# The gates of the first 128 tokens: one-hot products on TensorE, or indexed DMAs into a table in HBM

## The chip, the cores and the metric

The kernel runs on one core of one Trainium2 chip. The metric is the device time of one execution in microseconds (us), the median of several runs. TensorE (PE) multiplies matrices, VectorE (DVE) and ScalarE (ACT) work elementwise, GpSimd (POOL) and SyncE (SP) issue DMAs here. A profile row marked PEld is a weight load of TensorE.

## The reference, cut to what matters

A network of a hybrid mixer, an expert layer and two further layers on 256 tokens of width 1024, all in float32. The change is inside the expert layer: 8 heads each choose 16 of 128 x 128 experts for a token, and an expert is one row of `expert_u` and one of `expert_v`.

```python
v_half, i_half = lax.top_k(s, PEER_TOPK)
cand = (v_half[:, :, 0, :, None] + v_half[:, :, 1, None, :]).reshape(T, PEER_HEADS, PEER_TOPK * PEER_TOPK)
best, pos = lax.top_k(cand, PEER_TOPK)
i1 = jnp.take_along_axis(i_half[:, :, 0], pos // PEER_TOPK, axis=-1)
i2 = jnp.take_along_axis(i_half[:, :, 1], pos % PEER_TOPK, axis=-1)
experts = (i1 * PEER_KEYS + i2).reshape(T, PEER_HEADS * PEER_TOPK)
gates = jax.nn.softmax(best, axis=-1).reshape(T, PEER_HEADS * PEER_TOPK).astype(n.dtype)
...
u = expert_u[eb].astype(xb.dtype)
act = jax.nn.gelu(jnp.einsum('td,tkd->tk', xb, u), approximate=False) * gb
return jnp.einsum('tk,tkd->td', act, expert_v[eb].astype(xb.dtype))
```

## The kernel before, in words

All weights stream through the core once, as 523 chunks of 128 x 1024 floats (512 KB). SP issues each load into one of four buffers `raw`. ScalarE rounds it to `wh` and VectorE subtracts, `wl = raw - wh` (`pump_split`, L348); `wh` and `wl` have three buffers each, and the subtraction of a chunk is called its split below. A product is made of three: `wh` with the high part of the activations, `wh` with the low part, `wl` with the high part (`mm_a`, L424). So a chunk in the first expert stage is 24 matmuls of 256 columns, and the next load can be issued when the chunk four before it has been split.

The expert layer does not gather rows. Its **first stage** multiplies all tokens with all of `expert_u`: 128 chunks, one for each first index j, give 128 rows of activations `Hact` (tiles `hactA`, `hactB`), each 128 second indices by 256 tokens. Its **second stage** multiplies `Hact` with all of `expert_v`, again 128 chunks. What makes the result sparse is a gate for each expert and token, zero almost everywhere, by which gelu(`Hact`) is multiplied between the stages.

The gates come from work beside the stream. `topk1` (L1031) ranks the scores of a block of 128 tokens, `topk2` (L1040) ranks the sums, makes the gates `gt` and the two indices `isel`, and three TensorE transposes bring them to `idxT`. `g_side` (L1105) then takes four tokens at a time: ScalarE makes a one-hot tile `oA` of the first index, VectorE one of the second times the gate (`oB`), one float32 product for each token sums the 128 chosen experts into a gate table in PSUM (tile `sm`), and the table goes to `Hact`: where the row of activations is there already, VectorE multiplies it in, and where not, ScalarE copies the gates there, and `u_post` (L1200) multiplies gelu by them later.

`peer_side` (L1157) sets the order: `topk1(0)` and `topk2(0)` of tokens 0 to 127 first, then `g_side(0)` in turn with the ranking of tokens 128 to 255, then `g_side(1)`. Each part yields a cost, and each chunk of the stream grants it a rate, so these numbers pace the work:

```python
yield from paced(topk1(0), 1.3)
yield from paced(topk2(0), 1.3)
...
yield from paced(alternate(g_side(0), second()), 1.4)
yield from paced(g_side(1), 1.6)
```

The layer that records the program then orders each engine's instructions; every engine, and SP's queue, works through its own list in that order. `w_split` (L1231) splits two rows of `Hact` for the second stage.

Of the kernel before, what the change touches and what calls it, by code (L numbers as in the profile page):

```python
# [32 lines left out]
T0 = 16          # column of the first x token in the transposed activations (16 meta tokens precede)  # L33

# packed constants (from shapes alone)
# [3 lines left out]
def _consts():  # L39
# [11 lines left out]
    put("iota", np.broadcast_to(i[None, :], (128, 128)))  # L51
    first = off
# [19 lines left out]
# packed per-partition vectors  # L72
# [10 lines left out]
# the order of the mixer's products: gates (Z), steps (d), the groups of the scan, short convolution (S)  # L83
# [3 lines left out]
def half_order(nq):  # L87
    """The chunks (column half, place among the nq) of an output product before its last three: of a short
    one the second half starts early, as its last rows come late."""
    if nq == 4:  # L90
        return [(0, 0), (0, 1), (1, 0), (0, 2), (0, 3)]
    return [(0, i) for i in range(nq)] + [(1, i) for i in range(nq - 3)]


def layout(inp):
    """Lays the inputs out for the kernel: permutations, copies and concatenations only."""
    g = {k: np.asarray(v) for k, v in inp.items()}

    def A(w, c0):
        # 128 columns from c0, stationary: [128 d, kt, 128]  # L100
        w = w[:, c0:c0 + 128]
        return w.reshape(-1, 128, 128).transpose(1, 0, 2).reshape(128, -1)

    def Bc(w, c0, q):
        # rows of k-tiles 2q, 2q+1, 512 columns from c0
        return w[q * 256:(q + 1) * 256, c0:c0 + 512].reshape(2, 128, 512).transpose(1, 0, 2).reshape(128, 1024)
# [97 lines left out]
def build(tc, a, out):  # L204
    nc = tc.nc
    top = ExitStack()
    with top:
# [5 lines left out]
        # one area for the buffers of all phases, cut by hand (in KiB per partition); row j of the  # L213
        # expert activations lies at j KiB
# [10 lines left out]
        def place(off, shape, dtype, name):  # L225
            """A tile at byte off of the area; it takes over from what lies there."""
# [10 lines left out]
        class Pool:  # L237
            """Cuts [lo, hi) KiB of the area; a name's tiles rotate over its bufs slots."""
# [55 lines left out]
        # ------------------------------------------------------------ first loads  # L294
# [34 lines left out]
        # ------------------------------------------------------------ the weight stream  # L329
# [47 lines left out]
        # ------------------------------------------------------------ work beside the stream  # L377
# [14 lines left out]
        def add_side(gen, rate=1.0):  # L392
            """A generator of work beside the stream: it yields what its last part costs (1 if nothing),
            and gets rate per chunk."""
# [28 lines left out]
        # ------------------------------------------------------------ products with streamed weights  # L423
# [8 lines left out]
        def wa(o, rh, rl, c0, n):  # L432
            """One stationary chunk: o[128 columns, n tokens]."""
# [10 lines left out]
        def wb(outs, xh, xl, k0, c0, first, last):  # L444
            """One moving chunk of two k-tiles: outs[t][128 tokens, 512 columns]."""
# [5 lines left out]
        # ------------------------------------------------------------ norms between the phases  # L451
        def rstd_of(ssq, n, width, np_=128, eps=EPS):
            """1/sqrt(ssq/width + eps) for [128, n] sums."""
# [4 lines left out]
            # h = -v/2; a first guess of v^-1/2 from the bits of v/2, then Newton's iteration to  # L458
            # float32's accuracy
# [18 lines left out]
        def tr_half(z, n, h, l, c0, np_=128):  # L478
            """z[tokens, 512] transposed into k-tiles 4n .. 4n+3 of the two parts."""
# [15 lines left out]
        def start_next(h, l, c0, nh, between):  # L495
            """The first nh chunks of the next phase, the first four k-tiles first."""
# [11 lines left out]
        def scale_of(s2, r):  # L508
            """r[128, 2] = rstd of the sums of the two blocks; returns r by columns on all partitions."""
# [11 lines left out]
        def out_phase(pool, xh, xl, c0, ks, res, sets, nh, rs=None):  # L521
            """res += x^T W (times rs by token) by column halves. The result times the gains of sets is
            transposed into their parts as it comes, and the next phase starts on the first of them; the
            scale of the norm is left to its readers. Returns the first products and the sums of squares."""
# [95 lines left out]
        # ============================================================ hybrid mixer  # L620
# [30 lines left out]
        # the first three chunks of z, one block of tokens after the other  # L651
# [31 lines left out]
        def dt_side(dtr):  # L683
# [17 lines left out]
            # log1p(e) = 2 atanh(z), z = e / (2 + e) in (0, 1/3]  # L701
# [29 lines left out]

        def ssd_group(g):
# [5 lines left out]
            # s0  # L738
# [10 lines left out]
            # s1  # L749
# [22 lines left out]
            # s2  # L772
# [16 lines left out]
            # s3  # L789
# [4 lines left out]
            # s4  # L794
# [6 lines left out]
            # s5  # L801
# [6 lines left out]
            # s6  # L808
# [16 lines left out]
            # s7  # L825
# [4 lines left out]
            # s7, s8  # L830
# [7 lines left out]
            # gate, norm within the group  # L838
# [75 lines left out]
        def sc_chunks(i):  # L914
            # the convolution reaches two tokens back
# [24 lines left out]

        z_chunk()
# [25 lines left out]
        # ============================================================ PEER  # L967
# [6 lines left out]
        def Hact(j0, j1, t0, t1):  # L974
            """Rows j0 .. j1 of the expert activations for tokens t0 .. t1, in pieces: rows and tokens
            from the start of the range, and the piece."""
# [19 lines left out]
        idxT = tp.tile([128, 3, 256], F, name="idxT")  # L996
        ust = {"J": 0, "T": 0, "sc": set(), "topk": -1}
# [42 lines left out]
        def topk2(tb):  # L1040
# [5 lines left out]
            # of the sums of two falling lists only those of ranks r, s with (r + 1)(s + 1) <= 16 can be  # L1046
# [644 lines left out]
```

## Time and profile before

| | us |
|---|---|
| median of three runs (lowest, highest) | 1706.02 (1705.64, 1706.15) |
| span of the profiled execution | 1704.0 |
| first expert stage, about | 281 to 707 |
| block 0's products (tokens 0 to 127) | within 364 to 584 |
| second expert stage, about | 707 to 1107 |

The span runs from the first to the last instruction of the profiled execution; the runs' times hold some 2 us around it. An engine's list is worked through in order, so a row with idle time before it names what the engine waited for. A product of four tokens' one-hot tiles shows as eight records, two for each.

### The profile page before, as it was taken

What the parts mean: (1) busy time and instruction counts of PE and PEld (TensorE: products, weight loads), DVE (VectorE), ACT (ScalarE), POOL (GpSimd) and SP (SyncE); (2) the same over time, 40 slices, a digit from 0 to 9 for tenths busy, and PEclk for the clock granted to TensorE, in tenths of its full rate; (3) what the DMA queues carried; (4) which work ended last, traced back from release to release, by engine and by line L of the source; (5) the groups of instructions that cost most, each with busy time, mean ns of one, the idle gap of its engine ahead of it and who ended that gap; (6) DMA issues with size and microseconds to landing.
All of it is one profiled execution on the core that took longest, in us unless ns stands there. A gap on an engine that the chain in (4) does not pass through costs nothing. (4 is left out here: it accounts for less than half of the span.)

```text
span 1704.0 us, 29681 instructions
## 1 busy us (share of the span) xinstructions
PE 1683.1 (99%) x11373; PEld 1529.4 (90%) x11373; DVE 1271.0 (75%) x2529; ACT 1018.4 (60%) x1784; POOL 0.2 (0%) x4
## 2 busy tenths in 40 slices
PE   8999999999999999999999999999999999999998
PEld 6999889999999999988888888898899988799986
DVE  6789778989985699855555565887787757777754
ACT  6877456568885698644444555733555545665543
POOL 0000000000000000000000000000000000000000
PEclk9999999999999999999999999999999999999999
DMA  6444465554446544455555585533465655256553
GB/s 210 142 132 128 156 214 171 167 180 137 137 154 185 169 149 143 155 185 186 187 192 188 189 311 187 171 123 118 139 191 186 187 176 169 76 171 187 184 183 117
DMA packets 80959, 286.82 MB, mean 168 GB/s; under 512 B 9121, under 2 KB 11681, under 8 KB 80562
## 3 DMA queue, kind: packets, MB, share of 16 engines
q1 hardware_dynamic: 80818, 284.94, 52.8%
q8 instruction: 89, 1.46, 0.3%
q14 instruction: 52, 0.43, 0.1%
HBM read 282.80 MB, written 2.10 MB: 167 GB/s over the span
## 5 line engine op out<-in xcount | busy, mean ns | idle before, releaser
L271 DVE TENSOR_TENSOR wl<-raw,wh 128x1024 fp32r<-128x1024 f32 x523 | 638.7, 1222 | 295.8 <-ACT wh L283 293.4
L283 ACT ACTIVATE wh<-raw 128x1024 fp32r<-128x1024 f32 x523 | 551.7, 1057 | 425.9 <-PE acc L265 404.1
L265 PE MATMUL acc<-xTh,wh 128*128 128x256 f32 (+2 forms) x2184 | 543.9, 287 | 0.2 <-ACT xTh L283 0.2
L265 PE MATMUL acc<-xTl,wh 128*128 128x256 f32 (+2 forms) x2184 | 534.3, 282 | 1.0 <-DVE xTl L271 1.0
L265 PEld LDWEIGHTS acc<-xTl,wh 128*128 128x128 f32 x2184 | 412.5, 189 | 2.5 <-DVE xTl L271 1.2
L265 PEld LDWEIGHTS acc<-xTh,wh 128*128 128x128 f32 x2184 | 411.7, 189 | 3.2 <-issue 1.7
L265 PE MATMUL acc<-xTh,wl 128*128 128x256 f32 (+2 forms) x2184 | 306.8, 281 | 0.0
L265 PEld LDWEIGHTS acc<-xTh,wl 128*128 128x128 f32 x2184 | 279.8, 188 | 0.3 <-issue 0.3
L265 PE MATMUL acc<-wh,wth 128*128 128x512 f32 x512 | 201.8, 394 | 0.0
L265 PE MATMUL acc<-wl,wth 128*128 128x512 f32 x512 | 201.7, 394 | 0.0
L265 PE MATMUL acc<-wh,wtl 128*128 128x512 f32 x512 | 161.7, 394 | 0.0
L265 PEld LDWEIGHTS acc<-wh,wth 128*128 128x128 f32 x512 | 95.7, 187 | 23.9 <-issue 0.3
L265 PEld LDWEIGHTS acc<-wh,wtl 128*128 128x128 f32 x512 | 95.7, 187 | 23.6
L265 PEld LDWEIGHTS acc<-wl,wth 128*128 128x128 f32 x512 | 95.8, 187 | 23.6
L283 ACT ACTIVATE oA<-cst,idxT 128x128 f32<-128x128 f32 x256 | 83.9, 393 | 3.6 <-DVE idxT L1102 2.8
L277 DVE TENSOR_SCALAR oB<-cst,idxT 128x128 f32<-128x128 f32 x256 | 71.5, 341 | 1.1 <-PE sm L265 1.0
L265 PE MATMUL sm<-oB,oA 128*128 128x128 f32 x512 | 68.2, 276 | 4.1 <-DVE sw L1026 2.0
L265 PE MATMUL acc<-wl,fh 128*128 128x512 f32 x176 | 69.4, 394 | 0.0
L265 PE MATMUL acc<-wh,fh 128*128 128x512 f32 x176 | 69.4, 394 | 0.0
L265 PE MATMUL acc<-wh,fl 128*128 128x512 f32 x176 | 69.4, 394 | 0.0
L265 PEld LDWEIGHTS sm<-oB,oA 128*128 128x128 f32 x512 | 62.4, 191 | 5.7 <-ACT hactB L283 5.3
L283 ACT ACTIVATE wth<-hactA 128x512 fp32r<-128x512 f32 x48 | 30.3, 632 | 60.7 <-PE acc L265 58.4
(318 smaller groups left out, 2084.7 us busy)
## 6 DMA issues: line engine op xcount, KB each, us to landing
raw<-in_u SPq DMA_DIRECT2D x128, 512.0 KB, 3.6
raw<-in_v SPq DMA_DIRECT2D x128, 512.0 KB, 3.5
raw<-in_up SPq DMA_DIRECT2D x88, 512.0 KB, 3.6
raw<-in_w_in SPq DMA_DIRECT2D x45, 512.0 KB, 3.6
raw<-in_dn SPq DMA_DIRECT2D x44, 512.0 KB, 3.6
raw<-in_hg_in SPq DMA_DIRECT2D x32, 512.0 KB, 3.6
raw<-in_w_out SPq DMA_DIRECT2D x16, 512.0 KB, 3.6
raw<-in_w_q SPq DMA_DIRECT2D x16, 512.0 KB, 3.8
```

Source lines behind the costliest of these rows:

```text
L265: PE.matmul(o, l, r, start=start, stop=stop_)
L271: V.tensor_tensor(out=o, in0=x, in1=y, op=op)
L277: V.tensor_scalar(o, x, s1, s2, op0=op0, op1=op1)
L283: S.activation(o, i, f, **kw)
```

## The change

Tokens 128 to 255 keep their one-hot products. For tokens 0 to 127 `topk2` computes the place of each gate in a table `gtab` of 128 tokens x 128 x 128 floats in HBM (8 MB), from a new constant column `row`, the token's number. `scatter` issues 128 indexed DMAs on POOL, each of which adds one gate for each token (128 rows of 4 bytes) at its place. The 16 DMAs of a head go to different places; those of a later head may meet the same ones, so a head waits for the head before it. The table is written with zeros during the mixer, in 16 writes of 512 KB on SP (`zero_side`). `u_post` now writes gelu of tokens 0 to 127 straight to `Hact`. `g_load` reads the gates of two rows of `Hact` back (128 x 256 floats, two buffers `gts`), and `w_split` multiplies them in. The ranking of tokens 128 to 255 no longer alternates with products, and the rates change. Comments are left out too.

```diff
+        gtab = dram.tile([128 * 128 * 128, 1], F, name="gtab")
+        gtv = gtab.rearrange("(a c) o -> a (c o)", a=128)
+        zero = m2.tile([128, 256], F, name="zero", bufs=1)
+        V.memset(zero, 0.0)
+        def zero_side():
+            for i in range(16):
+                yield
+                SP.dma_start(gtv[:, i * 1024:(i + 1) * 1024].rearrange("a (k c) -> a k c", k=4),
+                             zero[:, None, :].to_broadcast([128, 4, 256]))
...
+        add_side(zero_side(), 0.5)
...
-        ust = {"J": 0, "T": 0, "sc": set(), "topk": -1}
+        gplace = tp.tile([128, 128], I32, name="gplace")
+        gval = tp.tile([128, 8, 16], F, name="gval")
+        ust = {"J": 0, "T": 128, "sc": set(), "topk": -1}
...
-            gt = tp.tile([128, 8, 16], F, name="gt")
+            gt = gval if tb == 0 else tp.tile([128, 8, 16], F, name="gt")
...
+            if tb == 0:
+                pl = ihf.rearrange("p (s h) r -> p s (h r)", s=2)[:, 0]
+                flat = lambda t: t.rearrange("p h r -> p (h r)")
+                ts(pl, flat(isel[:, 0]), -16384.0, C("row"), OP.mult, OP.add)
+                stt(gplace, flat(isel[:, 1]), 128.0, pl, OP.mult, OP.add)
+                scatter()
+                return
...
+        def after(ins, others):
+            for other in others:
+                tc.add_manual_dep(ins.ins, other.ins.name, mybir.DependencyInfo(
+                    mybir.DependencyClass.Sync, mybir.DependencyReason.DATA), reason="the same places")
+        def scatter():
+            for h in range(8):
+                before, head = list(last), []
+                for r in range(16):
+                    c = slice(h * 16 + r, h * 16 + r + 1)
+                    ins = nc.gpsimd.indirect_dma_start(
+                        out=gtab, out_offset=bass.IndirectOffsetOnAxis(ap=gplace[:, c].bitcast(U32), axis=0),
+                        in_=gval[:, h, r:r + 1], in_offset=None, compute_op=OP.add)
+                    for other in head:
+                        tc.declare_no_dep(ins.ins, other.ins, reason="other places")
+                    after(ins, before)
+                    head.append(ins)
+                last[:] = head
...
-            def second():
-                yield from topk1(1)
-                yield from topk2(1)
-            yield from paced(alternate(g_side(0), second()), 1.4)
-            yield from paced(g_side(1), 1.6)
+            yield from paced(topk1(1), 1.1)
+            yield from paced(topk2(1), 1.1)
+            yield from paced(g_side(1), 1.25)
...
-                if T > 0:
-                    act(pp[:, :, :T], pp[:, :, :T], AF.Gelu)
+                if T > 128:
+                    act(pp[:, :, 128:T], pp[:, :, 128:T], AF.Gelu)
...
-                for _, tsl, hv_ in Hact(2 * j2, 2 * j2 + 2, T, 256):
-                    act(hv_, pp[:, :, T + tsl.start:T + tsl.stop], AF.Gelu)
+                for t0, t1 in ((0, 256),) if T == 128 else ((0, 128), (T, 256)):
+                    for _, tsl, hv_ in Hact(2 * j2, 2 * j2 + 2, t0, t1):
+                        act(hv_, pp[:, :, t0 + tsl.start:t0 + tsl.stop], AF.Gelu)
...
+        gtp = Pool(144, AREA, 2)
+        gts = {}
+        def g_load(j2):
+            gts[j2] = gtp.tile([128, 2, 128], F, name="gts")
+            after(SP.dma_start(gts[j2].rearrange("p j t -> p (j t)"), gtv[:, j2 * 256:(j2 + 1) * 256]), last)
+        g_load(0)
+        g_load(1)
...
         def w_split(j2):
+            g = gts.pop(j2)
+            for _, tsl, hv_ in Hact(2 * j2, 2 * j2 + 2, 0, 128):
+                tt(hv_, hv_, g, OP.mult)
+            if j2 + 2 < 64:
+                g_load(j2 + 2)
```

The order on VectorE where block 0's selection ends, before (`cdw` and `ih` hold the selection, `idxT` the transposed indices, `wl<-raw,wh` is a split):

```order
L1024 MAX vh<-scores 128x8 x2
L271 TENSOR_TENSOR wl<-raw,wh 128x1024
L1024 MAX vh<-scores 128x8 x3
L271 TENSOR_TENSOR cdw<-vh 128x8x8
L271 TENSOR_TENSOR cdw<-vh 128x8x5
L271 TENSOR_TENSOR cdw<-vh 128x8x4
L271 TENSOR_TENSOR cdw<-vh 128x8x3
L271 TENSOR_TENSOR cdw<-vh 128x8x6
L271 TENSOR_TENSOR wl<-raw,wh 128x1024 x6
L1102 COPY idxT<-tr 128x3x128
L1025 MAX_INDEX ih<-vh,scores 128x8
L277 TENSOR_SCALAR oB<-cst,idxT 128x128 x8
```

And with the change:

```order
L272 TENSOR_TENSOR wl<-raw,wh 128x1024
L272 TENSOR_TENSOR cdw<-cdw,ihf 128x512
L1041 MAX_INDEX ih<-vh,scores 128x8
L1112 TENSOR_REDUCE ih<-cdw 128x32
L1042 MATCH_REPLACE sw<-vh,scores 128x128
L281 SCALAR_TENSOR_TENSOR gplace<-ih,ihf 128x128
L272 TENSOR_TENSOR wl<-raw,wh 128x1024
L1044 MAX vh<-sw 128x8
L1041 MAX_INDEX ih<-vh,scores 128x8
```

The transposed indices are gone, the places `gplace` follow the last selection of block 0, and the ranking of block 1 (MAX, MAX_INDEX, MATCH_REPLACE) comes there at once, where before six splits followed each other and `oB` tiles came next.

The order on SP's queue at the end of the sub-key loads and through the expert stages, before:

```order
L344 DMA raw<-in_w_q 128x1024
L1172 DMA qs<-in_sk 128x128
L344 DMA raw<-in_u 128x1024 x128
L344 DMA raw<-in_v 128x1024 x98
L1260 DMA hold<-hsp 128x2048
L344 DMA raw<-in_v 128x1024 x2
L1261 DMA cst_10670<-in_cst 128x1408
```

And with the change, behind the first 109 loads of u (waits for semaphores shown; DMASW are those of POOL's DMAs, DMAHW those of SP's):

```order
L345 DMA raw<-in_u 128x1024 [waits DMAHW1_49,DVE_49]
L1268 DMA gts<-gtab 128x256 [waits DMASW4_49,DMASW3_49,DMASW5_49,DMASW2_49,DMASW6_49,DMASW1_49,DMASW7_49,DMASW0_49,PE_49]
L345 DMA raw<-in_u 128x1024 [waits DMAHW2_49,DVE_49]
L1268 DMA gts<-gtab 128x256
L1268 DMA gts<-gtab 128x256 [waits DMAHW6_49,DVE_49]
L345 DMA raw<-in_u 128x1024 [waits DMAHW3_49,DVE_49]
L1268 DMA gts<-gtab 128x256 [waits DMAHW0_49,DVE_49]
```

The first table load stands behind the 110th load of u and waits for POOL's DMAs and for TensorE; from there on table loads stand between the weight loads.

The order on VectorE at the same place, from the 107th split of u on, before:

```order
L271 TENSOR_TENSOR wl<-raw,wh 128x1024
L271 TENSOR_TENSOR hactA<-sm,hactA 128x4x96
L271 TENSOR_TENSOR hactB_7136<-sm,hactB_7136 128x4x8
L277 TENSOR_SCALAR oB<-cst,idxT 128x128 x4
L271 TENSOR_TENSOR hactB_4359<-acc,hactB_4359 128x256
L271 TENSOR_TENSOR hactB_7136<-acc,hactB_7136 128x2x52
L271 TENSOR_TENSOR wl<-raw,wh 128x1024
```

And with the change:

```order
L272 TENSOR_TENSOR wl<-raw,wh 128x1024
L272 TENSOR_TENSOR hactA<-sm,hactA 128x4x96
L272 TENSOR_TENSOR hactB_5902<-sm,hactB_5902 128x4x8
L272 TENSOR_TENSOR hactB_5902<-acc,hactB_5902 128x2x124
L272 TENSOR_TENSOR hactA<-hactA,gts 128x2x128
L272 TENSOR_TENSOR wl<-raw,wh 128x1024
L272 TENSOR_TENSOR wtl<-hactA,wth 128x512
L272 TENSOR_TENSOR hactA<-hactA,gts 128x2x128 x2
```

The `oB` tiles are gone, and the first multiplication by a table row stands between the 107th split and the 108th, two more behind the 108th; the list goes on so to the 64th.

POOL has no DMA before. With the change its list holds 128 indexed DMAs; the first ones with their waits:

```order
L1141 DMA gtab<-gval,gplace 2097152x1 [waits DMAHW4_49,DMAHW3_49,DMAHW5_49,DMAHW2_49,DMAHW6_49,DMAHW1_49,DMAHW7_49,DMAHW0_49,DVE_49]
L1141 DMA gtab<-gval,gplace 2097152x1 x7
L1141 DMA gtab<-gval,gplace 2097152x1 [waits DMASW0_49]
L1141 DMA gtab<-gval,gplace 2097152x1 [waits DMASW1_49]
L1141 DMA gtab<-gval,gplace 2097152x1 [waits DMASW2_49]
L1141 DMA gtab<-gval,gplace 2097152x1 [waits DMASW3_49]
L1141 DMA gtab<-gval,gplace 2097152x1 [waits DMASW4_49]
L1141 DMA gtab<-gval,gplace 2097152x1 [waits DMASW5_49]
L1141 DMA gtab<-gval,gplace 2097152x1 [waits DMASW6_49]
L1141 DMA gtab<-gval,gplace 2097152x1 [waits DMASW7_49]
L1141 DMA gtab<-gval,gplace 2097152x1 [waits DMASW4_49,DMASW5_49,DMASW3_49,DMASW6_49,DMASW2_49,DMASW7_49,DMASW1_49,DMASW0_49]
```

Eight DMAs go out on eight semaphores, each of the next eight waits for the one eight before it, and the 17th, the first of the next head, waits for all of them; this repeats for eight heads.

## Rows read from the trace of the kernel before

**Rows 1.** The page: busy time by engine, then tenths of it in 40 slices.

```profile
PE 1683.1 (99%) x11373; PEld 1529.4 (90%) x11373; DVE 1271.0 (75%) x2529; ACT 1018.4 (60%) x1784; POOL 0.2 (0%) x4
...
PE   8999999999999999999999999999999999999998
DVE  6789778989985699855555565887787757777754
POOL 0000000000000000000000000000000000000000
PEclk9999999999999999999999999999999999999999
DMA  6444465554446544455555585533465655256553
```

**Rows 2.** Stretches of the span; columns are in the first row.

```profile
core 0: us, PE busy (x) PEld busy (x) DVE busy (x) ACT busy (x) POOL busy (x), PEclk, DMA share, GB/s
20.00:180.00 160.00, 159.96 (x1166) 149.26 (x1165) 132.47 (x282) 121.65 (x222) 0.00 (x0) 1.00 0.46 143
281.00:364.00 83.00, 83.00 (x705) 83.00 (x705) 74.47 (x229) 43.94 (x59) 0.00 (x0) 1.00 0.58 179
364.00:584.00 220.00, 215.93 (x1828) 214.56 (x1827) 179.28 (x491) 165.82 (x358) 0.00 (x0) 1.00 0.51 157
584.00:707.00 123.00, 122.96 (x1054) 122.76 (x1053) 115.69 (x248) 109.11 (x261) 0.00 (x0) 1.00 0.47 142
707.00:1107.00 400.00, 398.62 (x1872) 326.45 (x1872) 242.01 (x302) 203.97 (x261) 0.00 (x0) 1.00 0.60 199
```

**Rows 3.** Groups by line, 364 to 584; after | busy us, mean ns, then idle before.

```profile
L265 PE MATMUL sm<-oB,oA 128*128 128x128 f32 x256 | 34.4, 277 | 4.1 <-DVE sw L1026 2.0 <-ACT hactB L283 1.5 <-DVE oB L277 0.6
...
L265 PEld LDWEIGHTS sm<-oB,oA 128*128 128x128 f32 x256 | 31.2, 191 | 5.4 <-ACT hactB L283 5.3
...
L277 DVE TENSOR_SCALAR oB<-cst,idxT 128x128 f32<-128x128 f32 x128 | 35.7, 340 | 0.0
```

**Rows 4.** Order of time, weight loads, 371 to 373; start us, us.

```profile
371.14 1.02 PEld L265 LDWEIGHTS acc<-xTh,wl 128*128 128x128 f32 x8
372.08 0.98 PEld L265 LDWEIGHTS sm<-oB,oA 128*128 128x128 f32 x8
372.98 0.19 PEld L265 LDWEIGHTS acc<-xTh,wh 128*128 128x128 f32 x1
```

**Rows 5.** Order of time, VectorE, 348 to 361; start us, us, idle before.

```profile
348.14 0.66 DVE L1096 TENSOR_REDUCE ih<-cdw 128x32 f32<-128x512 f32 x1
...
349.12 1.20 DVE L271 TENSOR_TENSOR wl<-raw,wh 128x1024 fp32r<-128x1024 f32 x1
...
354.27 1.23 DVE L271 TENSOR_TENSOR wl<-raw,wh 128x1024 fp32r<-128x1024 f32 x1 [0.40 <-ACT wh L283]
357.11 1.22 DVE L271 TENSOR_TENSOR wl<-raw,wh 128x1024 fp32r<-128x1024 f32 x1 [1.61 <-ACT wh L283]
359.95 1.23 DVE L271 TENSOR_TENSOR wl<-raw,wh 128x1024 fp32r<-128x1024 f32 x1 [1.62 <-ACT wh L283]
```

**Rows 6.** Groups by line, VectorE, 281 to 364.

```profile
L271 DVE TENSOR_TENSOR wl<-raw,wh 128x1024 fp32r<-128x1024 f32 x29 | 35.2, 1216 | 8.1 <-ACT wh L283 8.1
```

**Rows 7.** The sub-key loads on SP, all 16, then the seven from 256 on.

```profile
L1172 SPq DMA_DIRECT2D qs<-in_sk x16: 328/400/1721, 239.8 to 271.1; - x16
...
DMA to landing us min/median/max: 1.7/4.1/7.2
...
L1172 SPq DMA_DIRECT2D qs<-in_sk x7: 328/328/358, 256.2 to 271.1; - x7
...
DMA to landing us min/median/max: 1.7/2.3/2.7
```

**Rows 8.** Groups by line, VectorE, 977 to 1067.

```profile
L271 DVE TENSOR_TENSOR wtl<-hactB,wth 128x256 fp32r<-128x256 f32 x32 | 13.4, 423 | 3.2 <-PE acc L265 3.2
```

**Rows 9.** The page: DMA issues, KB each, median us to landing.

```profile
raw<-in_u SPq DMA_DIRECT2D x128, 512.0 KB, 3.6
raw<-in_v SPq DMA_DIRECT2D x128, 512.0 KB, 3.5
```

More of the change, by code (lines that the diff above doesn't have):

```diff
@@ L51, in _consts @@
     put("iota", np.broadcast_to(i[None, :], (128, 128)))
+    put("row", i[:, None])
     first = off
@@ L995, in build @@
         ihf = tp.tile([128, 16, 16], F, name="ihf")
-        idxT = tp.tile([128, 3, 256], F, name="idxT")
-        ust = {"J": 0, "T": 0, "sc": set(), "topk": -1}
+        idxT = tp.tile([128, 3, 128], F, name="idxT")
+        gplace = tp.tile([128, 128], I32, name="gplace")
+        gval = tp.tile([128, 8, 16], F, name="gval")
+        ust = {"J": 0, "T": 128, "sc": set(), "topk": -1}
         scores = Pool(112, 128).tile([128, 32, 128], F, name="scores")
@@ L1101, in topk2 @@
             yield
-            V.tensor_copy(idxT[:, :, tb * 128:(tb + 1) * 128],
-                          pt[:, :384].rearrange("p (j t) -> p j t", j=3))
+            V.tensor_copy(idxT, pt[:, :384].rearrange("p (j t) -> p j t", j=3))
+        last = []
+        def after(ins, others):
[15 more added lines that the diff above has]
+                last[:] = head
         def g_side(tb):
@@ L1132, in g_side @@
                         t = t4 * 4 + j
+                        t -= tb * 128
                         act(oA[:, j], iota, AF.Square, bias=idxT[:, 0, t:t + 1])
@@ L1141, in g_side @@
                 yield 1.2 + 0.004 * ust["J"]
-        def alternate(g1, g2):
-            gens = [g1, g2]
-            while gens:
-                for g in list(gens):
-                    try:
-                        c = next(g)
-                        yield c
-                    except StopIteration:
-                        gens.remove(g)
         def paced(gen, rate):
@@ L1202, in f1 @@
                 T = ust["T"]
-                if T > 0:
-                    act(pp[:, :, :T], pp[:, :, :T], AF.Gelu)
+                if T > 128:
+                    act(pp[:, :, 128:T], pp[:, :, 128:T], AF.Gelu)
                     def f2():
-                        for _, tsl, hv_ in Hact(2 * j2, 2 * j2 + 2, 0, T):
-                            tt(hv_, pp[:, :, tsl], hv_, OP.mult)
+                        for _, tsl, hv_ in Hact(2 * j2, 2 * j2 + 2, 128, T):
+                            tt(hv_, pp[:, :, 128 + tsl.start:128 + tsl.stop], hv_, OP.mult)
                     post(1, f2)
-                for _, tsl, hv_ in Hact(2 * j2, 2 * j2 + 2, T, 256):
-                    act(hv_, pp[:, :, T + tsl.start:T + tsl.stop], AF.Gelu)
+                for t0, t1 in ((0, 256),) if T == 128 else ((0, 128), (T, 256)):
+                    for _, tsl, hv_ in Hact(2 * j2, 2 * j2 + 2, t0, t1):
+                        act(hv_, pp[:, :, t0 + tsl.start:t0 + tsl.stop], AF.Gelu)
                 ust["J"] = 2 * j2 + 2
@@ L1226, in build @@
         wp = Pool(128, 136, 2)
-        spare[333] = Pool(136, AREA)
+        spare[333] = Pool(136, 144)
+        gtp = Pool(144, AREA, 2)
[5 more added lines that the diff above has]
+        g_load(1)
         pacc = [bank("acc") for _ in range(4)]
```

## The prediction

> **What bounds the kernel now.** I read the page's shares first, then the table of stretches, then the groups and the order of time inside the stretch that the change touches. TensorE is busy 99% of the span and POOL does nothing [rows 1]. In the first expert stage (281 to 707) TensorE has 4.1 us of idle time in all, and all but 0.04 us of it lies between 364 and 584 [rows 2]. So this stage lasts as long as TensorE's instructions: what leaves TensorE there comes off the time, as long as nothing else becomes late. VectorE is next: 90% busy from 281 to 364, 81% from 364 to 584, 94% from 584 to 707 [rows 2]. The clock is 1.00 throughout. The profiled execution has a span of 1704.0 us; the median of the three runs is 1706.02, so I add 2.0 for what lies around the span. A measurement of this kernel can tell about 0.2% (3.4 us) from no change.
>
> **The change, part by part.**
>
> *Products that leave TensorE.* Each token of a block has one product of its two one-hot tiles, recorded as two matmuls. Block 0's 256 records lie all in 364 to 584 [rows 3]. Their price is the step in the weight loads: a group of four tokens begins at 372.08 and the next chunk at 372.98, so 0.90 us [rows 4]. 32 groups x 0.90 = **28.8 us**. The group's own busy time (34.4 us as matmuls, 31.2 as weight loads [rows 3]) counts overlap with neighbours twice, so I take 28.8 and keep 34.4 as the far end. The rest of the queue closes up, since weight loads follow each other without a wait.
>
> *Waits that go with them.* The same groups show 4.1 us of idle time before block 0's products (5.4 on the load side), which wait for VectorE's ranking of block 1 and for ScalarE's copies [rows 3]. Block 1's products alone, from 584 on, show 0.04 us of idle time [rows 2]. I take **4.1 us** off.
>
> *Ranking of tokens 128 to 255, now without pauses.* It moves ahead of all products, so VectorE carries it in about 25 chunks from 349 on. A chunk lasts 2.84 us (splits at 354.27, 357.11, 359.95 [rows 5]), 25 of them 71 us. The nearest row is block 0's ranking: 74.5 us of VectorE in 281 to 364, of which 35.2 are the 29 splits [rows 2, 6], so 39.3 for a ranking and what lies beside it. 39.3 plus 25 splits at 1.22 are 69.8 us of 71: just covered, with splits that would come late in the denser first half. I charge **2 us**, bounds 0 and 8.
>
> *Indexed DMAs.* 128 of them stand on POOL, behind the places (`gplace`), which follow block 0's last selection at 349 [rows 5]. The order shows when they must be done: SP puts the first table load behind the 110th u load, and VectorE's first multiplication by a table row stands behind split 107. The split at 349.12 is the 22nd, so this is 85 chunks x 2.84 = 241 us later, plus block 1's 28.8 us of products: at 619. Until then nobody waits for POOL: **270 us of cover, 2.1 us for each DMA**, with some 5 us more in the two splits by which VectorE runs ahead. If the cover is gone, the table load blocks SP, all weight loads queue behind it, VectorE stands in its own queue before the next split, and TensorE starves: every further us is lost whole. No row shows a DMA from POOL. The nearest is the load of sub-keys, also 128 small rows among weight loads: 0.40 us to issue, 4.1 us to land (1.7 to 7.2) [rows 7]. Low end: 128 x 0.33 and a landing of 1.7 per head, 56 us. High end: each alone from issue to landing, 128 x 4.1 = 525 us. The order of POOL allows eight in flight and closes a head with a full landing, so I take 8 x (16 x 0.40 + 4.1) = 84 us, a third of the cover: **0 us**, far end 525 - 270 - 5 = 250 us.
>
> The Trainium skill speaks against this step. SBUF — State Buffer, section "A bandwidth-pool intuition that's wrong (but worth ruling out)", says that a DMA issued from GpSimd which takes about 620 ns alone takes about 3100 ns beside a VectorE copy, because POOL cannot write its descriptors while VectorE holds their shared port. By that figure, an estimate, the 128 DMAs take 397 us, end at 746, and the sum below would be 1677 + 122 = 1799 us; by the rows on SP's queue it is 1677. No run shown here has a DMA on POOL, so neither is borne out yet.
>
> *Table loads and multiplications.* 64 loads of 128 KB on SP, two buffers, and 64 multiplications of 128 x 256 on VectorE: the nearest is a subtraction of that shape, 423 ns [rows 8], so 27 us in all. They stand at up to two to a chunk from split 107 on, where products have ended: 1.22 + 2 x 0.42 + about 0.4 for block 1's own multiplication is 2.5 of 2.84 us, hidden by TensorE. But the next pair of loads is issued only after the pair before is used, so a pair costs 0.42 us plus a landing. 44 multiplications in the 25 chunks from there to the second stage's first splits leave 3.2 us for a pair. Late sub-key loads land in 2.3 us [rows 7], weight loads of four times the size in 3.6 [rows 9]; at 2.6 us a pair takes 3.0 and fits, at 4.1 it takes 4.5, and 22 pairs lose 29 us less 5 of lead. I charge **2 us**, bounds 0 and 24. In the second stage VectorE is busy 242 of 400 us [rows 2] and a pair has two chunks: nothing.
>
> *Zeroing the table.* 16 writes of 512 KB among the 45 loads of w_in. These loads keep the DMA engines 46% busy in 20 to 180 [rows 2]; 61 for 45 makes 62%, and each load has four chunks to land. 0 us. ScalarE's one-hot tiles and VectorE's go too (35.7 us on VectorE [rows 3]), with gelu of tokens 0 to 127 now written straight to its row: off the path, 0.
>
> **Sum:** 1704.0 - 28.8 - 4.1 + 2 + 2 = 1675.1, and 2.0 around it: **1677 us**, 1.7% faster. With both charges at zero, 34.4 for the products and 5.4 for the waits it is 1666; with 8 and 10 charged, 1691. That is the likeliest case's own range.
>
> **The rivals.**
>
> *POOL comes late (slower).* If POOL can issue only while VectorE is idle, the cover shrinks: VectorE is idle 40.7 of 220 us, 18.5% [rows 2], so 50 of the 270 us. It decides at an issue of 0.39 us. At twice SP's 0.40, POOL needs 102 us, has 50 by 619, and does the other 52 while VectorE stands blocked; less 5 us of lead that is 47 lost: **1724 us**. The fully serial end is 1677 + 250 = 1927. For it: VectorE is the engine with the least slack here, each DMA has 128 separate rows that add to HBM, and POOL must read each list of places. Against it: a factor of three between 84 and 270. The skill's port rule named above is of this kind. Chance 0.32.
>
> *The loop of table loads is too slow.* Landing at 4.1 us as sub-keys do at the median, the 22 pairs give back 24 us instead of 2: **1699 us**. For it: each load queues behind a 512 KB weight load. Against it: 2.3 us for the seven late sub-key loads [rows 7]. Chance 0.10.
>
> **How the numbers follow.** The forecast's case has 0.58, and is faster in all of its range. POOL late: 0.26 slower, 0.02 the same, 0.04 faster. Slow loop: 0.04 faster, 0.04 the same, 0.02 slower. Together faster 0.66, same 0.06, slower 0.28. The range begins at 1665; to hold eight in ten it must reach over the slow loop and about half of POOL's case, whose priced point is 1724: I end it at 1740.
>
> **What would show it.** Right: no one-hot products from 364 to 475 and chunks there at 2.84 us; TensorE's idle time in the stage under 5 us; the last indexed DMA issued long before 619, and table loads with no wait for POOL; the second stage starting some 30 us earlier. POOL's late case shows one long idle stretch on TensorE near split 107, with SP's first table load waiting for POOL's DMAs. The slow loop shows splits spaced 3.5 to 4.5 us instead of 2.84 between the 107th and the end of the stage, each ended by a landing of `gts`. Splits above 2.84 us between 349 and 420 would prove my charge for the ranking too small. The forecast is wrong if TensorE's gaps in the stage exceed 15 us.

## The result, and the profile after

The changed kernel takes **1713.83 us** (median of 4 runs, 1713.63 to 1717.77) beside 1705.97 before on the same chip: 1.0052 times as long, 95% interval 1.0039 to 1.0064. It is 0.5% slower, where 1677 was forecast. The profiled execution has a span of 1711.8 us in a run of 1713.63.

The page's busy times after, with TensorE, VectorE and POOL in tenths of 40 slices and the granted clock:

```profile
PE 1664.1 (97%) x11114; PEld 1508.7 (88%) x11114; DVE 1229.0 (72%) x2380; ACT 947.4 (55%) x1582; POOL 233.2 (14%) x132
...
PE   8999999999999978799999999999999999999998
...
DVE  6789778999478845665555565897787757877754
...
POOL 0000000068787770000000000000000000000000
PEclk9999999999999998999999999999999999999999
```

TensorE lost 19 us of work against [rows 1] and still ends later: its row has a dent of 7 8 7 in the middle that was not there. POOL, empty before, works from the 9th to the 15th slice, and the dent begins where POOL ends. The stretches say how much is missing; the first five answer to [rows 2]:

```profile
core 0: us, PE busy (x) PEld busy (x) DVE busy (x) ACT busy (x) POOL busy (x), PEclk, DMA share, GB/s
20.00:180.00 160.00, 159.96 (x1165) 149.26 (x1164) 132.44 (x282) 121.58 (x222) 0.00 (x0) 1.00 0.63 197
281.00:364.00 83.00, 83.00 (x705) 83.00 (x704) 79.74 (x285) 43.99 (x59) 12.34 (x7) 1.00 0.57 168
364.00:584.00 220.00, 217.95 (x1833) 216.16 (x1832) 168.74 (x383) 147.02 (x303) 174.61 (x94) 1.00 0.72 169
584.00:707.00 123.00, 100.03 (x809) 97.33 (x807) 69.54 (x122) 59.00 (x117) 46.08 (x29) 0.93 0.63 161
707.00:1107.00 400.00, 392.84 (x1786) 321.16 (x1787) 244.58 (x319) 197.12 (x251) 0.00 (x0) 0.99 0.64 206
...
620.00:650.00 30.00, 12.92 (x102) 12.72 (x101) 5.63 (x10) 4.00 (x9) 19.16 (x13) 0.74 0.33 41
...
650.00:750.00 100.00, 88.89 (x586) 80.19 (x585) 62.36 (x100) 41.43 (x58) 0.00 (x0) 0.96 0.75 227
```

There are three losses. From 620 to 650 TensorE stands still for 17 of 30 us. From 650 to 750, where the last chunks of the first expert stage and the first of the second lie, 11 us are missing in many small gaps. And between 364 and 584, where 4.1 us were idle before, 2.1 still are, now beside VectorE's ranking and not beside the products. The write of zeros costs nothing: 20 to 180 has the same 159.96 us of TensorE as before.

In order of time, the end of the indexed DMAs on POOL, the first table load on SP, and the first multiplication by a table row on VectorE (start us, us, idle before):

```profile
641.27 1.54 POOL L1141 DMA_INDIRECT gtab<-gval,gplace  x1 [0.30 <-issue]
```

```profile
617.31 0.33 SPq L345 DMA_DIRECT2D raw<-in_u  x1
644.34 0.33 SPq L1268 DMA_DIRECT2D gts<-gtab  x1
644.77 0.38 SPq L345 DMA_DIRECT2D raw<-in_u  x1
```

```profile
622.01 0.41 DVE L272 TENSOR_TENSOR hactB<-acc,hactB 128x248 f32<-128x248 f32 x1
646.38 0.42 DVE L272 TENSOR_TENSOR hactA<-hactA,gts 128x256 f32<-128x256 f32 x1 [23.95 <-DMA gts<-gtab]
```

SP issues a weight load at 617.31, then stands in front of the table load until 644.34, and so the next weight load comes at 644.77. VectorE waits 23.95 us, with the next split behind that multiplication, and TensorE waits 17.08 us for that split:

```profile
647.99 2.08 PE L266 MATMUL acc<-xTh,wl 128*128 128x256 f32 x8 [17.08 <-DVE wl L272]
```

The groups by line of POOL and VectorE (busy us, mean ns, idle before) and SP's waits (us in total, times, longest) name both waits:

```profile
L1141 POOL DMA_INDIRECT gtab<-gval,gplace x128 | 233.0, 1821 | 409.4 <-DVE gplace L281 349.4 <-issue 36.8 <-DMA gtab<-gval,gplace 23.1
L272 DVE TENSOR_TENSOR hactA<-hactA,gts 128x256 f32<-128x256 f32 x48 | 19.9, 425 | 56.6 <-DMA gts<-gtab 56.1
L272 DVE TENSOR_TENSOR hactB<-hactB,gts 128x256 f32<-128x256 f32 x16 | 6.8, 424 | 11.4 <-DMA gts<-gtab 11.3
```

```profile
SPq L1268 <- DMA gts<-gtab: 35.1, 34, 2.1
SPq L1268 <- DMA gtab<-gval,gplace: 26.5, 4, 21.1
```

POOL needs 233.0 + 36.8 + 23.1 = 293 us, from 349.8 to 642.8: 2.29 us for each DMA, where the cover is 2.1. Of VectorE's 67 us of waits for table rows, 24 are the first; the other 43 are the loop of loads.

### The profile page after: what moved, and what is told of

It reads as the page before. It is cut to its first block, busy times and chain, and to the rows that moved or that the text cites. A ratio compares the mean times of both kernels' runs of the same rounds, so it can differ in the third digit from the quotient of the medians.

```text
span 1711.8 us, 29074 instructions
## 1 busy us (share of the span) xinstructions
PE 1664.1 (97%) x11114; PEld 1508.7 (88%) x11114; DVE 1229.0 (72%) x2380; ACT 947.4 (55%) x1582; POOL 233.2 (14%) x132
## 5 line engine op out<-in xcount | busy, mean ns | idle before, releaser
L266 PE MATMUL acc<-xTh,wl 128*128 128x256 f32 (+2 forms) x2184 | 310.5, 284 | 25.1 <-DVE wl L272 24.9
L1141 POOL DMA_INDIRECT gtab<-gval,gplace x128 | 233.0, 1821 | 409.4 <-DVE gplace L281 349.4
L272 DVE TENSOR_TENSOR hactA<-hactA,gts 128x256 f32<-128x256 f32 x48 | 19.9, 425 | 56.6 <-DMA gts<-gtab 56.1
L272 DVE TENSOR_TENSOR wtl<-hactA,wth 128x512 fp32r<-128x512 f32 x48 | 33.1, 690 | 26.5 <-ACT wth L284 26.5
L266 PE MATMUL acc<-wh,xTh 128*128 128x512 f32 x112 | 47.3, 423 | 0.7 <-ACT wh L284 0.7
```

What stands on the lines that cost most here:

```text
L266: PE.matmul(o, l, r, start=start, stop=stop_)
L272: V.tensor_tensor(out=o, in0=x, in1=y, op=op)
L1141: ins = nc.gpsimd.indirect_dma_start(out=gtab, out_offset=bass.IndirectOffsetOnAxis(ap=gplace[:, c].bitcast(U32), axis=0), in_=gval[:, h, ...
```

## The experiments

Medians of four or five runs, in us; the kernel before, run beside each group of experiments, took 1705.92 to 1706.29.

| run | what it does | us | ratio, 95% |
|---|---|---|---|
| changed kernel | | 1713.83 | 1.0039 to 1.0064 |
| e1_other_source | table loads read an input | 1713.72 | 1.0026 to 1.0060 |
| e9_lists_apart | e1, and the lists lie elsewhere | 1696.77 | 0.9928 to 0.9961 |
| e2_no_scatter | no indexed DMAs | 1691.06 | 0.9894 to 0.9927 |
| e11_seven_heads | 112 of 128 indexed DMAs | 1691.12 | 0.9897 to 0.9933 |
| e3_no_table | no DMAs, loads, multiplications | 1675.50 | 0.9804 to 0.9837 |
| e4_late_loads | first load held late | 1689.43 | 0.9886 to 0.9919 |
| e5_paced_loads | each load paced | 1682.86 | 0.9850 to 0.9883 |
| e6_ten_buffers | late, ten buffers | 1681.13 | 0.9837 to 0.9870 |
| e7_paced_rank | e5, ranking paced | 1678.87 | 0.9822 to 0.9855 |
| e10_held_products | ranking paced, multiplications held | 1671.62 | 0.9786 to 0.9813 |

### What the parts cost: no table, no indexed DMAs

e3_no_table drops `scatter()`, the `g_load` calls and the four lines that multiply in `w_split`; e2_no_scatter drops the first of these alone:

```
             if tb == 0:
...
-                scatter()
                 return
```

> Neither indexed DMAs nor table loads nor the multiplications by the table (the gates of the first 128 tokens are left out); the removed one-hot products, the denser ranking and the zero writes stay as in the changed kernel. Theory (products and their waits give back 28.8 + 4.1, the denser ranking takes about 5): 1706.0 - 32.9 + 5 = about 1678. Rival (removed products were partly hidden, or the ranking takes more): 1685 to 1700.

> No indexed DMA at all, loads and multiplications of the table stay as they are and read zeros (the gates of the first 128 tokens are left out). If the indexed DMAs cost nothing but the wait, it comes within 2 us of the run whose loads read another source, about 1696. If their traffic or their descriptors also slow the rest of the first expert stage, it lies 5 us or more below that run.

They take 1675.50 and 1691.06 us. Without the table the change gives 30.5 us, near what the products and their waits were priced at. The difference between the two runs, **15.6 us**, is the loop of loads and multiplications; what is left to the changed kernel, 1713.83 - 1691.06 = **22.8 us**, is all that the indexed DMAs cost. e2_no_scatter lies 5 us below my 1696, which took the loop at 19 us.

### Is it the wait alone? Another source, and lists apart

```
-            after(SP.dma_start(gts[j2]..., gtv[:, j2 * 256:(j2 + 1) * 256]), last)
+            SP.dma_start(gts[j2]..., a["v"][:, j2, :256])
```

> The table loads read an input weight of the same size, so they no longer wait for the 128 indexed DMAs, which still run (the gates of the first 128 tokens are left out). Theory (two separate losses: the wait of the first load for the last indexed DMA, 17.5 us of idle TensorE, and the loop of table loads, about 19 us): the first goes, the second stays, 1713.8 - 17.5 = about 1696, and less by a few us more if the half-clock stretch behind the gap goes with it. Rival (the loop alone decides, it would fall behind whenever it starts): 1708 to 1714.

It takes 1713.72 us: no gain at all, and the time that I had put down for the rival. But the rival's reason does not hold either, as VectorE's order of time in this run shows:

```profile
624.60 0.43 DVE L272 TENSOR_TENSOR hactA<-hactA,gts 128x256 f32<-128x256 f32 x1 [1.59 <-DMA gts<-in_v]
624.94 1.22 DVE L272 TENSOR_TENSOR wl<-raw,wh 128x1024 fp32r<-128x1024 f32 x1
645.85 0.69 DVE L272 TENSOR_TENSOR wtl<-hactA,wth 128x512 fp32r<-128x512 f32 x1 [19.69 <-DMA gtab<-gval,gplace]
```

The first multiplication now runs at 624.60, and then VectorE waits 19.69 us for the indexed DMAs all the same, in front of `wtl`. That tile takes over the space at 128 KiB in which `gplace` and `gval` lie, and POOL's DMAs read those two to their end. There are two waits for the same event, one behind the other. e9_lists_apart moves the lists to space that the second stage takes over only at its end:

```
-        tp = Pool(128, AREA)
-        gp = tp
+        tp, gp = Pool(128, 134.25), Pool(134.25, AREA)
...
-        gplace = tp.tile([128, 128], I32, name="gplace")
-        gval = tp.tile([128, 8, 16], F, name="gval")
+        gp.tile([128, 8, 64], F, name="cdw", bufs=1)
+        gplace = gp.tile([128, 128], I32, name="gplace")
+        gval = gp.tile([128, 8, 16], F, name="gval")
```

> As the run whose loads read another source (1713.7), but the two lists that the indexed DMAs read, places and values, lie outside the space that the second stage's buffers wth and wtl take over (the gates of the first 128 tokens are left out). Theory (that run kept its wait because wtl takes over the lists' space, and so also waits for the last indexed DMA): the wait goes, 1691 within 2 us, as without indexed DMAs. Rival (the indexed DMAs slow the stage in another way, by traffic or descriptors): above 1700.

It takes 1696.77 us: 17 us go, so the second wait was real. It misses my 1691 by 6. In its profile the loop runs beside the last indexed DMAs until 644 and TensorE has 86.59 us between 650 and 750, against 88.88 without indexed DMAs. VectorE's waits for the loads are longer, 49.8 us against 43.6. They are longer in e1_other_source too, 47.2 us behind the first against 43.4 in the changed kernel, although nearly all of its loop runs after the last indexed DMA; so the other source of the loads is the likelier reason, but no run separates the two.

### How sharp is the edge? Seven heads

```
-            for h in range(8):
+            for h in range(7):
```

> The changed kernel with seven of the eight heads written to the table (112 indexed DMAs; the gates of the eighth head of the first 128 tokens are left out). In the changed kernel the eighth head takes 612.3 to 642.8, and SyncE comes to its first table load at about 619. Theory (a cliff: all that ends before about 619 is free, what ends later is lost whole): the seventh head's last DMA ends at about 608, so the whole wait goes and the loop's cost stays: 1691 within 2. Rival (the indexed DMAs also cost while they are covered, in proportion): 1713.8 - 22.7/8 = about 1711.

It takes 1691.12 us, the time without any indexed DMA. 112 of them cost nothing that these runs can tell, and the last 16 cost 22.7 us. SP's order of time in this run shows where the edge lies:

```profile
616.63 0.33 SPq L345 DMA_DIRECT2D raw<-in_u  x1
619.85 0.33 SPq L1268 DMA_DIRECT2D gts<-gtab  x1
620.36 0.33 SPq L345 DMA_DIRECT2D raw<-in_u  x1
```

The first table load is issued at 619.85; the cover in the prediction ended at 619. With all eight heads it is issued 24.5 us later.

### What sets the pace of an indexed DMA

e8_scatter_alone and e12_scatter_beside are kernels of their own, run once each; only their traces are used.

> A kernel of its own that computes nothing of the reference: five stages of 32 indexed DMAs of 128 single elements, with made-up places: alone; beside a stream of 512 KB weight loads; beside VectorE subtractions of 128x1024 float32; beside both; alone without the addition. Theory (the transfers of others stretch an indexed DMA, VectorE doesn't): about 1.55 us each alone and beside VectorE, 1.8 to 2.4 beside the stream. Rival (VectorE shares something with GpSimd): 1.55 beside the stream, 1.8 to 2.4 beside VectorE. Without the addition: no expectation, 1.0 to 1.6.

My theory fell: POOL's group of 32, stage by stage (alone; beside the stream; beside VectorE's subtraction; without the addition), reads

```profile
L249 POOL DMA_INDIRECT gtab<-gval,gplace x32 | 49.8, 1558 | 39.7 <-DMA gtab<-zero 30.3 <-issue 9.4
...
L249 POOL DMA_INDIRECT gtab<-gval,gplace x32 | 49.7, 1553 | 11.6 <-issue 9.4 <-DMA gtab<-gval,gplace 2.1
...
L249 POOL DMA_INDIRECT gtab<-gval,gplace x32 | 70.7, 2209 | 11.7 <-issue 9.4 <-DMA gtab<-gval,gplace 2.2
...
L249 POOL DMA_INDIRECT gtab<-gval,gplace x32 | 31.1, 973 | 11.6 <-issue 9.5 <-DMA gtab<-gval,gplace 2.2
```

A stream that keeps the DMA engines 91% busy does nothing to it; VectorE's subtraction adds 0.65 us. (The stage beside both is left out: VectorE worked in only 12 of its 62 us.) e12_scatter_beside asks which work of VectorE does it.

> A kernel of its own that computes nothing of the reference: seven stages of 32 indexed DMAs, with made-up places, each beside one kind of work of VectorE on float32: none; subtraction of two tiles of 128x1024; product of two tiles of 128x256; a comparison with a column and a product on 128x128; a copy of 128x1024; the first eight of 128x512; the subtraction again with a stream of 512 KB loads. In the stages' run before, the subtraction stretched an indexed DMA from 1.55 to 2.21 us and the stream did nothing. Theory A (any work of VectorE stretches it): every stage but the first above 1.8. Theory B (only some kinds do, as the changed kernel's own indexed DMAs are longest beside its 128x1024 subtractions and not beside its comparisons): the two-tile stages at 2.0 or more, comparison and first-eight at 1.55 to 1.6; the copy is open. The last stage: 2.2, as without the stream.

POOL's groups beside: the subtraction of 128x1024, the product of 128x256, the copy of 128x1024, the subtraction with the stream:

```profile
L249 POOL DMA_INDIRECT gtab<-gval,gplace x32 | 70.7, 2209 | 11.6 <-issue 9.5 <-DMA gtab<-gval,gplace 2.2
...
L249 POOL DMA_INDIRECT gtab<-gval,gplace x32 | 49.5, 1548 | 12.1 <-issue 9.4 <-DVE w L274 2.6
...
L249 POOL DMA_INDIRECT gtab<-gval,gplace x32 | 60.3, 1884 | 175.3 <-DVE w L278 165.9 <-issue 9.4
...
L249 POOL DMA_INDIRECT gtab<-gval,gplace x32 | 71.1, 2221 | 30.7 <-DVE w L281 21.3 <-issue 9.4
```

Beside nothing it is 1549 ns, beside the comparisons and the first-eight 1547 each. Theory B seems to hold, but for the 128x256 product, which has two tiles too and seems to do nothing. The changed kernel shows the same difference: of its 128 indexed DMAs, the 28 that overlap no 128x1024 subtraction of a weight split take 1553 ns on average, at most 1600; the 33 that overlap one for 1.1 us or more take 2080, at most 2574.

But some of those 33 take no more than 1545. What decides is whether VectorE's instruction is already running when the indexed DMA starts. Here are two DMAs of the changed kernel on POOL, and the split beside each on VectorE:

```profile
428.81 1.55 POOL L1141 DMA_INDIRECT gtab<-gval,gplace  x1 [0.30 <-issue]
...
435.67 2.53 POOL L1141 DMA_INDIRECT gtab<-gval,gplace  x1 [0.31 <-issue]
```

```profile
429.90 1.23 DVE L272 TENSOR_TENSOR wl<-raw,wh 128x1024 fp32r<-128x1024 f32 x1 [1.39 <-ACT wh L284]
...
435.56 1.23 DVE L272 TENSOR_TENSOR wl<-raw,wh 128x1024 fp32r<-128x1024 f32 x1 [1.61 <-ACT wh L284]
```

The split at 429.90 starts during the DMA and costs it nothing. The split at 435.56 has 1.12 us left when the DMA starts, and the DMA takes 0.99 us more. Over all 128 the rule read from these rows holds: 1.545 us, and on top whatever of a VectorE instruction with both inputs in SBUF remains at the start, less 0.126 us. It gives 115 of the 128 times within 0.01 us and 125 within 0.06. Sums that read `sm` or `acc` from PSUM do not count: the DMA at 568.47 starts with 0.85 us of one left and takes 1.55.

The size of the instruction matters only through what can be left of it. At 407.87 a 128x512 comparison of two tiles in the selection has 0.62 us left, and the DMA takes 2.04; at 390.80 a 128x128 one has 0.24 left, and the DMA takes 1.66. In the stage beside the 128x256 product the first DMA starts with 0.18 us of a product left and takes 1.60; all the others start with less than 0.12 us left or between two products, so that stage does not show that a small product is harmless.

So an indexed DMA costs POOL 1.55 + 0.30 us, and up to 1 us more where a split is running at its start; these holds are 35 of POOL's 293 us. Without them, 128 x 1.55 + 36.8 + 23.1 = 258 us, an estimate, the last would end at 608, in time.

The Trainium skill, SBUF — State Buffer, section "Who interferes with whom", says that a VectorE instruction with two inputs in SBUF contends with a GpSimd instruction that reads SBUF. The 2.53 us beside a running split and the 2.04 beside a running 128x512 comparison agree. The section infers that such an instruction does not stall a DMA's descriptors; here the indexed DMA was held all the same, and no run shows whether in reading its places or in writing its descriptors.

### What the loop of loads costs, and where it need not

e4_late_loads lets the first load go only after a late split (`spl[i]` keeps the instruction of split i); e5_paced_loads has `spl[200 + 2 * j2]` in its place; e6_ten_buffers is e4 with `gtp = Pool(136, AREA, 10)` and loads ten pairs ahead:

```
-            after(SP.dma_start(...), last)
+            after(SP.dma_start(...), last + [spl[200]])
```

> Everything computed; only the first table load may not be issued before the split of the 200th streamed chunk, six chunks before the first expert stage ends, so that the last indexed DMA lies behind it and the loop of loads runs beside the second expert stage. Theory (wait and loop cost because they fall into the last 20 chunks of the first stage): the wait of 17.5 us goes, the loop's delays move to where VectorE has room; 1678 + 2 to 6 = 1680 to 1684. Rival (the loop of two buffers costs its 19 us wherever it runs): about 1697.

> Everything computed; the table load of pair j waits for the split of chunk 200 + 2j, so that the 64 loads come one per two chunks through the second expert stage rather than as fast as two buffers allow. Theory (the loop of loads costs 14 to 15 us because SyncE, unpaced, spends its time in it and issues the weight loads late): that cost goes, and the time comes to that of the kernel without the table, 1675.5, plus at most 3: 1676 to 1679. Rival (two buffers and a landing of 3 us per pair cost the time wherever they run): 1687 to 1690, as with the loads held late but unpaced.

> Loads held late as in the run that had 1689.4, unpaced, but with ten buffers for them instead of two. Theory (SyncE stands waiting for VectorE to free one of two buffers): most of the 14 us goes, 1677 to 1681. Rival (not the buffers but the crowd of loads ahead of the weight loads makes the weights late): 1685 to 1690.

They take 1689.43, 1682.86 and 1681.13 us. Holding the first load late takes away the wait for POOL, but 13.9 of the loop's 15.6 us stay: it costs in the second stage as well, and my theory of the place was wrong. Pacing leaves 7.4 us and ten buffers 5.6, which is 3.9 and 0.1 us above what I had expected of them at most. VectorE's groups tell what is left; paced, then with ten buffers:

```profile
L272 DVE TENSOR_TENSOR hactA<-hactA,gts 128x256 f32<-128x256 f32 x48 | 20.4, 426 | 108.9 <-DMA gts<-gtab 108.9
L272 DVE TENSOR_TENSOR hactB<-hactB,gts 128x256 f32<-128x256 f32 x16 | 6.8, 425 | 30.8 <-DMA gts<-gtab 30.7
```

```profile
L272 DVE TENSOR_TENSOR hactA<-hactA,gts 128x256 f32<-128x256 f32 x48 | 18.8, 420 | 15.3 <-DMA gts<-gtab 15.3
```

Paced, the multiplication stands so early in VectorE's order that VectorE waits 139.6 us in front of loads that have not landed, and splits wait behind it. e10_held_products leaves two buffers and the late first load, and instead holds each multiplication to the chunk it is written beside; like e7 it also holds the ranking (next part):

```
-                tt(hv_, hv_, g, OP.mult)
+                after(V.tensor_tensor(out=hv_, in0=hv_, in1=g, op=OP.mult), [spl[st["split"] - 1]])
```

> Everything computed; ranking held to its chunks as in the run that had 1678.9, the first load held late, and instead of pacing the loads each multiplication by the table waits for the split of the chunk it is written beside, so VectorE no longer stands in front of a table load that has not landed (139 us of such waits in the paced run). Theory (what is left of the loop's cost, 7 us against the run without a table, is VectorE waiting at the head of its queue, splits behind it): 1675.5 - 4.0 + 1 = about 1672. Rival (the loads' place in SyncE's queue ahead of the weights is what costs): 1677 to 1680.

It takes 1671.62 us. The group is down to

```profile
L1285 DVE TENSOR_TENSOR hactA<-hactA,gts 128x256 f32<-128x256 f32 x48 | 20.3, 424 | 1.6
```

with no wait for a load at all, and TensorE is busy 100.00 us of 700 to 800. With the 4.0 of the ranking (next part) added back it is 1675.6, the time without a table: the loop costs nothing beyond the runs' spread when VectorE is not put in front of a load. It is also the fastest kernel here, 2.0% faster than the one before (0.9786 to 0.9813), with the indexed DMAs all in it.

### The ranking of tokens 128 to 255

e7_paced_rank is e5 with a wait on the last split for V.max in `top16` and for the comparison in the selection:

```
+        def held(tb, ins):
+            if tb == 1:
+                after(ins, [spl[st["split"] - 1]])
...
-                V.max(out=vals[:, 0:8], in_=src)
+                held(tb, V.max(out=vals[:, 0:8], in_=src))
```

> Paced loads as in the run before it in this call; besides, the ranking of tokens 128 to 255 is held to the chunk it is written beside, by a wait on the last split, since its rate alone does not hold it (VectorE takes it as soon as its inputs are there). Theory (TensorE's 4 to 5 us of gaps between 372 and 420 us come from that crowd on VectorE): 4 to 5 us less than that run, about 1673. Rival (gaps move with the ranking): no difference, within 1.5 us.

It takes 1678.87 us, **4.0 us** less than e5; the four runs of each spread over 3 to 4 us, so the profile has to bear it out. The stretch from 350 to 450, first in the changed kernel, then in this run:

```profile
350.00:450.00 100.00, 97.95 (x810) 96.16 (x808) 86.14 (x273) 46.66 (x54) 82.30 (x44) 1.00 0.77 182
```

```profile
350.00:450.00 100.00, 100.00 (x848) 100.00 (x847) 85.64 (x277) 48.77 (x56) 80.20 (x44) 1.00 0.80 193
```

VectorE does the same work in it, 86 us, and TensorE's gaps are gone: 2.05 us of matmuls, 3.84 on its weight loads (96.16 against 100.00). The rate 1.1 in the change does not hold the ranking back: VectorE takes it as soon as its inputs are there, crowded into the chunks from 349 to 424, with light ones behind until 479.

## Why the prediction was wrong

*Products, their waits, zeroing, ranking: right.* These terms alone gave 1677 - 2 for the loop = 1675; without the table the kernel takes 1675.50. The ranking cost 4.0 where I charged 2, inside my bounds, and as named: splits come 3.1 to 3.6 us apart from 369 to 386. Products and waits then brought 1706.0 + 4.0 - 1675.5 = 34.5, against 32.9. The two misses cancel, so the match to half a us is partly luck.

*Indexed DMAs, "0 us": the step that failed.* The place and the cover were right: SP comes to the first table load at 619 and there are 2.1 us for each DMA. The price was wrong, and with it the end of the last DMA and TensorE's gaps: they are 23 us between 584 and 707, where I had named 15 as the sign of being wrong. I took 84 us from the sub-key loads on SP, 0.40 us to issue each [rows 7], because they are also 128 small rows; POOL takes 1.55 to 2.57 us for one, 0.30 between two, and 3.3 (23.1 / 7) for the landing between two heads. No row of before bounded this price, and "a third of the cover" sounded safer than it was. With the measured 293 us my own sum gives 293 - 270 - 5 of lead = 18 us, and TensorE's gap is 17.08. The whole loss is 22.8: behind the gap TensorE worked 3.51 us at a granted clock of 0.50, which is some 1.8 more by estimate; the rest I did not take apart.

*The rival that came true* is "POOL comes late": one long idle stretch on TensorE near split 107, SP's first table load waiting for POOL, as described. I priced it at 1724 by letting POOL work only while VectorE is idle. In fact it works on beside VectorE, and is held only at the start of a DMA, by what is left of a split: 18 us by the sum above, not 47. The figure of the Trainium skill, SBUF — State Buffer, section "A bandwidth-pool intuition that's wrong (but worth ruling out)", some 3100 ns beside a VectorE copy instead of 620 alone, has a larger factor than the runs: 1884 beside a copy and 1549 alone here. Its reason, that POOL waits until VectorE's instruction is over, agrees with the order of time above; the port itself no run shows. It told that the price is not that of a DMA on SP, and I gave it too little weight.

*The loop of loads, "2 us": the second failure.* It cost 15.6 us, inside my 0 to 24. I did name the pair that waits for its landing, and took 2.6 us for a landing; it is 3.0 to 3.1 at the median. Chunks then take 3.5 us on average, not 2.84, from the 109th to the 133rd split. And "in the second stage: nothing" holds only if the multiplications stand late enough: held late but not paced, the loop cost 13.9 there too.

*The sum in hindsight:* 1675.5 + 15.6 + 22.8 = 1713.9. The last two terms are differences of runs, so that this comes out shows nothing by itself. I had two slow rivals as alternatives; they happened together. The measured time lies inside the range, but the direction I forecast was wrong. That 1713.8 is so near to the rival's 1724 is luck: its wait was priced too high, and the loop beside it too low.

## What to carry to other kernels

Price an operation that no row of the profile shows by a small run of its own, beside the work that it will run beside, and not by its nearest namesake on another queue. Work off the path is free up to the moment at which somebody comes for it, and then nearly every microsecond counts: 112 indexed DMAs cost nothing, and with the next 16 the first load came 24.5 us later and the kernel took 22.7 us longer. And a wait can stand in a place that the code does not show: after the loads' own wait was gone, the reuse of the lists' space kept it, and an engine that was put in front of a load too early held up all that stood behind.

## What the runs showed of the hardware

- An indexed DMA with addition of 128 single elements keeps POOL 1.55 us, without addition 0.97, and 0.30 us pass before the next. A stream at 298 GB/s does not change it (1553 ns). An instruction on VectorE with both inputs in SBUF that is running when it starts adds what is left of it, less 0.13 us (0.99 us for 1.12 left); one that starts during it adds nothing. A running 128x1024 copy adds about all that is left of it: the first DMA of that stage starts with 0.47 us left and takes 2.01.
- TensorE's granted clock fell behind the gap of 17.08 us, and also behind one of 2.44 us. Three stretches of the changed kernel (one that is mostly that shorter gap, what follows, and a while later):

```profile
716.80:719.75 2.95, 0.57 (x4) 0.25 (x3) 1.98 (x4) 1.71 (x3) 0.00 (x0) 1.00 0.80 258
719.75:723.17 3.42, 3.36 (x8) 2.69 (x9) 2.33 (x5) 0.00 (x0) 0.00 (x0) 0.50 0.79 242
...
730.00:740.00 10.00, 10.00 (x45) 8.09 (x44) 6.58 (x11) 4.35 (x6) 0.00 (x0) 1.00 0.70 203
```

After a stretch in which TensorE worked 0.57 of 2.95 us, the granted clock is 0.50, the lower of its two levels (1.2 GHz), and 8 matmuls take the 3.4 us in which at 1.00 there is room for some 15 (45 in 10 us). So this gap of the loop cost more than its own length.
